# Two steps of the projections per round, in the stage that prepares the delta rule's chunks

## The chip, the cores and the metric

The kernel runs on one core of a Trainium2 chip. A core has a matrix engine (TensorE, PE in the profile), a vector engine (VectorE, DVE), a scalar engine (ScalarE, ACT), GpSimd (POOL) and a queue engine (SyncE, SP) that issues most DMAs. Each engine works through its own list of instructions in order; semaphores make an instruction wait for others. The metric is the time on the device, in microseconds (us), of one execution; a median of several is given.

## The reference

The program is one encoder layer for 1024 tokens of width 1024, with adaptive scale and shift. `hmix @ w_in` gives the inputs of three mixers: a gated short convolution (256 channels), a neighbourhood attention (4 heads of 64) and a gated delta rule in both directions (4 heads of 128). Their outputs go through `w_out`; then a router sends every token to 2 of 32 experts, and a last norm ends it. All is float32; a product that needs the precision is made of three matmuls over high and low parts.

```
proj = hmix @ w_in[l]
y_conv = cb * _dwconv(cc * cx, conv_a_w[l])
y_na = _neighbourhood_attention(...)
y_gdn = _gdn_mixer(gqkv, gz, ga, gb, ...)       # chunks, triangular solve, scan; times silu(gz)
mixed = concatenate([y_conv, y_na, y_gdn]) @ w_out[l]
x = x + gate1 * mixed
y_moe = _hier_moe(rmsnorm(x), ...)
```

The delta rule needs, per chunk, the inverse of a unit triangular matrix, and then walks over the chunks one after the other with a state, once forward and once backward.

## The kernel before

The sequence is cut into 8 chunks of 128 tokens. The stages in time: input norm and first projections; attention beside the delta rule's own projections (to about 365 us); then the stage of the change; then `w_out`, second norm and router; then, from about 860 us, the experts.

What the change touches is the list of generators at lines 806 to 815. Each generator emits some instructions and yields; one such piece is called a step here. `rounds` (line 120) goes round: one step of every generator it has, in the order given, until those named in `until` are through. What is left of the others goes on in the next call of `rounds`, at line 920.

- `prep_as` (lines 735 and 683), two generators with four chunks each, 7 steps a chunk: loads, decay matrices, norms, transposes and two products of each chunk, and stores to DRAM; the last (line 731) is the transposed triangular matrix `l_d`. So its 28 steps stand in rounds 1 to 28.
- `prj` (lines 324 and 812): the projections that are left, with weights loaded on ACT's queue and split into a high and a low part on ACT and DVE (line 62). First six conv projections (`feat`, line 334, 8 steps each with 6 matmuls of 512 columns a step, line 340), then two groups of gate inputs z, 8 steps each (`tok`, line 346), one step a chunk of 128 tokens: 24 matmuls of 256 columns (line 355) and a readout by ACT and DVE and a store (lines 505 to 507). A step of `tok` is called a token step, or token, below; there are 16. Altogether `prj` has 64 steps.
- `pcs`: two generators of `prep_c` (line 774), one over chunks 0, 1, 2, 3, the other over 7, 6, 5, 4, 11 steps a chunk. They solve the matrix from blocks of 16 up to 128 in three steps of size (line 783). Each has masks on POOL and DVE (lines 787 to 789), a product copied to `Y` by ACT (line 792), and two more products added by DVE (lines 795 and 796). Then DVE scales the result into `to` (line 801), which is stored (line 802).
- `inverses`: `prep_b` (line 745), the 16 x 16 blocks, in two halves: chunks 0, 7, 1, 6 and then 2, 5, 3, 4. On DVE (lines 759 and 761), with nine steps each. The first waits for the second chunk of `prep_as`, the second for the fourth, so that they stand in rounds 14 to 22 and 28 to 36. `prep_c` of a chunk waits for its half.

The call at line 815 ends with `inverses`, after 37 rounds. The call at line 920 goes on with the rest of `prj`, `pcs`, two `visits` (line 843, the scan, which waits for `done_c` of its chunk) and `wo_thread` (line 904). The latter scales and splits a row block of `w_out` and writes it over the tiles `hh` and `hl` that the projections read; its row k is emitted once 9 + k token steps are.

The order of the code is not yet an engine's order. A planner goes through all instructions in a simulated time of its own. Where several are ready for one engine, it takes the one that was emitted first; where none of the early ones is ready, a later one goes ahead. Tiles of a pool share a fixed number of buffers: three PSUM banks `mm` for the projections, two `t1` tiles for what is read out of them.

Of the kernel before, what the change touches and what calls it, by code (L numbers as in the profile page):

```python
# [33 lines left out]
def body(tc, I, O):  # L34
    nc = tc.nc
    with ExitStack() as ctx:
        _body(ctx, tc, nc, I, O)


def _body(ctx, tc, nc, I, O):  # L40
# [79 lines left out]
    def rounds(*threads, until=None):  # L120

        live = list(threads)
        left = list(threads if until is None else until)
        while left:
            for g in list(live):
                if next(g, live) is live:
                    live.remove(g)
                    if g in left:
                        left.remove(g)
# [7 lines left out]
    def fast(g, n):  # L137

        for i, _ in enumerate(g):
            if i % n == n - 1:  # L140
                yield
# [161 lines left out]
    def chain(*gs, every=0):  # L303

        n = 0
        for g in gs:
            for _ in g:
                n += 1
                if every and n % every == 0:
                    tick()  # L310
                yield
# [7 lines left out]
    def proj(*items, got=(), q=sp):  # L319

        todo = [spec for specs, _ in items for spec in specs]
        got = [*got] or [wload(*spec, q) for spec in todo[:2]]
        n = len(got)
        for specs, f in items:
            ws = []
            for _ in specs:
                if n < len(todo):
                    got.append(wload(*todo[n], q))
                    n += 1
                ws.append(wsplit(got.pop(0)))  # L330
            yield from f(ws)
# [403 lines left out]
    def prep_as(cs):  # L735
        d = cs[0] // 7
        nxt = prep_load(cs[0], d)
        for i, c in enumerate(cs):
            f, R = nxt
            for n in prep_a(c, f, R):  # L740
                if n and i + 1 < len(cs):
                    nxt = prep_load(cs[i + 1], d)
                yield

    def prep_b(cs):

        while not done_a.issuperset(cs):
            yield
        N = g1p.tile([P, 2, 16, 16], F32, name="N")
        for i, c in enumerate(cs):  # L750
            for a in range(2):
                sp.dma_start(N[32 * i:32 * i + 32, a], blocks(l_d[c, a]))
        W = g1p.tile([P, 2, 16, 16], F32, name="W")
        pool.memset(W, 0.0)
        Wf = W.rearrange("p a i j -> p a (i j)")
        pool.memset(Wf[:, :, 0:256:17], 1.0)
        pr = g1p.tile([P, 2, 15, 15], F32, name="prod")
        for i in range(1, 16):
            dve.tensor_tensor(pr[:, :, :i, :i], N[:, :, i, None, :i].to_broadcast([P, 2, i, i]),
                              W[:, :, :i, :i].rearrange("p a j c -> p a c j"), op=OP.mult)  # L760
            dve.tensor_reduce(W[:, :, i, :i], pr[:, :, :i, :i], axis=AX.X, op=OP.add)
            if i % 2:
                yield
        pool.memset(Wf[:, 1, 0:256:17], 0.0)
        Z = g1p.tile([P, 2, 16, 16], F32, name="Z")
        pool.tensor_add(Z[:, 0], W[:, 0], W[:, 1].rearrange("p i j -> p j i"))
        pool.tensor_add(Z[:, 1], W[:, 1], W[:, 0].rearrange("p i j -> p j i"))
        for i, c in enumerate(cs):
            for a in range(2):
                sp.dma_start(blocks(t_d[c, a]), Z[32 * i:32 * i + 32, a])  # L770
        done_b.update(cs)
        yield

    def prep_c(c):
        while c not in done_b:
            yield
        LT = gc.tile(H4, F32, name="LT")
        sp.dma_start(LT, dense(l_d[c, 1]))
        TT = gc.tile([P, 2, 4, P], F32, name="TT")
        for a in range(2):  # L780
            sp.dma_start(TT[:, a], dense(t_d[c, a]))
        yield
        for s in (16, 32, 64):
            BT = gc.tile(H4, F32, name="BT")
            D1 = gc.tile(H4, F32, name="D1")
            D2 = gc.tile(H4, F32, name="D2")
            pool.tensor_mul(BT, LT, m4(f"b{s}"))
            dve.tensor_mul(D1, TT[:, 0], m4(f"m{s}"))
            pool.tensor_mul(D2, TT[:, 1], m4(f"m{s}"))
            yield  # L790
            Y = gc.tile(H4, F32, name="Y")
            act.copy(Y, mm4(BT, D1, psc))
            yield
            if s < 64:
                dve.tensor_add(TT[:, 0], mm4(D2, Y, psc), TT[:, 0])
            dve.tensor_add(TT[:, 1], mm4(Y, D2, psc), TT[:, 1])
            yield
        for d, n in ((0, "ui"), (1, "li"))[::1 if c < 4 else -1]:
            to = gc.tile(H4, F32, name="to")
            for h in range(4):  # L800
                dve.scalar_tensor_tensor(to[:, h], TT[:, 1, h], colv[:, 2, d, h, c:c + 1], M[n], op0=OP.mult, op1=OP.mult)
            sp.dma_start(w_d[c, d], flat(to))
        done_c.add(c)
        yield
# [6 lines left out]
    inverses = chain(prep_b((0, 7, 1, 6)), prep_b((2, 5, 3, 4)))  # L811
    prj = proj(*conv, *zs, q=act)
    pcs = [chain(*(prep_c(c) for c in halves[i::2])) for i in range(2)]
    pas = [prep_as(lo), prep_as(up)]
    rounds(*pas, prj, *pcs, inverses, until=[*pas, inverses])
    qctx.close()


# [1097 lines left out]
```

## Time and profile before

| | us |
|---|---|
| median of 3 runs | 1516.59 (1515.83 to 1517.48) |
| the profiled execution | 1518.59 |
| its span | 1516.8 |
| PE, DVE, ACT, POOL busy in the span | 1355.5, 1173.4, 804.9, 424.2 |
| the stage's `prep_a`, from its first load to its last store | 367 to 530 |
| `prep_c`, from its first load of a block inverse to its last store | 505 to 673 |

The profile is of one execution. A row of the timeline has the start, the duration, engine, line, operation and tiles, and, in brackets, how long the engine had been idle and what ended that. Neighbouring rows of one kind are merged, with their count behind an x. A name with q (SPq) is an engine's queue as it issues. Matmuls overlap, so the start of the next row says more of PE than the duration does.

### The profile page before, as it was taken

What the parts mean: (1) busy time and instruction counts of PE and PEld (TensorE: products, weight loads), DVE (VectorE), ACT (ScalarE), POOL (GpSimd) and SP (SyncE); (2) the same over time, 40 slices, a digit from 0 to 9 for tenths busy, and PEclk for the clock granted to TensorE, in tenths of its full rate; (3) what the DMA queues carried; (4) which work ended last, traced back from release to release, by engine and by line L of the source; (5) the groups of instructions that cost most, each with busy time, mean ns of one, the idle gap of its engine ahead of it and who ended that gap; (6) DMA issues with size and microseconds to landing.
All of it is one profiled execution on the core that took longest, in us unless ns stands there. A gap on an engine that the chain in (4) does not pass through costs nothing. (4 is left out here: it accounts for less than half of the span.)

```text
span 1516.8 us, 21838 instructions
## 1 busy us (share of the span) xinstructions
PE 1355.5 (89%) x7239; PEld 1076.5 (71%) x7239; DVE 1173.4 (77%) x2143; ACT 804.9 (53%) x1333; POOL 424.2 (28%) x294
## 2 busy tenths in 40 slices
PE   3988999999877888869999789999999999999983
PEld 2866777777766788868877678878866776676652
DVE  6758666544547688757877789999999889978996
ACT  3633454433544222321332367778888768767873
POOL 0011311200100555633532011212236414413432
PEclk9998999999998899989999689999999999999997
DMA  9496455223788676658565779999999999989923
GB/s 340 121 198 195 149 177 166 96 74 89 204 201 210 174 195 214 192 191 273 164 246 175 305 264 372 374 352 374 359 346 391 366 393 365 377 311 320 366 82 148
DMA packets 172601, 375.75 MB, mean 248 GB/s; under 512 B 33458, under 2 KB 99634, under 8 KB 147908
## 3 DMA queue, kind: packets, MB, share of 16 engines
q1 hardware_dynamic: 162500, 351.13, 67.7%
q0 software_dynamic: 7072, 16.73, 4.7%
q10 hardware_dynamic: 2912, 6.46, 1.4%
q8 instruction: 59, 0.97, 0.3%
q14 instruction: 58, 0.48, 0.1%
HBM read 325.38 MB, written 56.80 MB: 252 GB/s over the span
## 5 line engine op out<-in xcount | busy, mean ns | idle before, releaser
L62 DVE TENSOR_TENSOR wl<-w,wh 128x1024 fp32r<-128x1024 f32 (+1 forms) x392 | 456.7, 1195 | 33.8 <-ACT wh L62 30.9
L62 ACT CAST wh<-w 128x1024 fp32r<-128x1024 f32 (+1 forms) x392 | 401.0, 1033 | 118.7 <-PE y L1357 45.6
L1445 POOL DMA_INDIRECT x_d<-yo,ixp x27 | 127.0, 4704 | 222.8 <-DVE yo L1441 214.4
L340 PE MATMUL mm<-hh,wh 128*128 128x512 f32 x352 | 148.1, 421 | 0.0
L340 PE MATMUL mm<-hh,wl 128*128 128x512 f32 x352 | 143.3, 407 | 1.4 <-DVE wl L62 1.4
L340 PE MATMUL mm<-hl,wh 128*128 128x512 f32 x352 | 143.8, 409 | 0.0
L1368 PE MATMUL h<-wl,xh 128*128 128x512 f32 x288 | 122.8, 427 | 9.0 <-DVE wl L62 7.9
L1368 PE MATMUL h<-wh,xh 128*128 128x512 f32 x288 | 113.3, 401 | 0.7 <-ACT wh L62 0.7
L1357 PE MATMUL y<-wh,uh 128*64 128x512 f32 (+1 forms) x272 | 108.2, 398 | 0.8 <-ACT uh L62 0.5
L1357 PE MATMUL y<-wh,ul 128*64 128x512 f32 (+1 forms) x272 | 107.1, 394 | 0.4 <-DVE ul L62 0.4
L1357 PE MATMUL y<-wl,uh 128*64 128x512 f32 (+1 forms) x272 | 106.3, 398 | 0.7 <-DVE wl L62 0.7
L1357 PE MATMUL h<-wh,xh 128*128 128x512 f32 x224 | 90.3, 403 | 1.0 <-ACT u L1412 0.9
L1357 PE MATMUL h<-wl,xh 128*128 128x512 f32 x224 | 89.6, 400 | 0.0
L1357 PE MATMUL h<-wh,xl 128*128 128x512 f32 x224 | 88.5, 395 | 0.8 <-DVE xl L62 0.6
L1381 POOL DMA_INDIRECT oacc<-xn_d,ixp x29 | 50.2, 1732 | 134.7 <-PE pt L1397 117.8
L1368 PEld LDWEIGHTS h<-wl,xh 128*128 128x128 f32 x288 | 54.3, 189 | 40.3 <-DVE wl L62 31.6
L340 PEld LDWEIGHTS mm<-hh,wh 128*128 128x128 f32 x352 | 68.2, 194 | 18.2 <-issue 6.9
L340 PEld LDWEIGHTS mm<-hl,wh 128*128 128x128 f32 x352 | 68.2, 194 | 15.5 <-issue 0.3
L340 PEld LDWEIGHTS mm<-hh,wl 128*128 128x128 f32 x352 | 68.2, 194 | 13.4 <-DVE wl L62 1.7
L405 POOL TENSOR_TENSOR acc<-acc,wa 128x512 f32<-128x512 f32 x28 | 40.7, 1452 | 87.2 <-ACT wa L403 48.4
L1368 PEld LDWEIGHTS h<-wh,xh 128*128 128x128 f32 x288 | 54.4, 189 | 8.8 <-ACT wh L62 1.4
L1357 PEld LDWEIGHTS y<-wl,uh 128*64 128x64 f32 (+1 forms) x272 | 42.6, 157 | 20.9 <-DVE wl L62 2.4
(440 smaller groups left out, 3138.2 us busy)
## 6 DMA issues: line engine op xcount, KB each, us to landing
w<-we SPq DMA_DIRECT2D x192, 1024.0 KB
wa<-w_ada SPq DMA_DIRECT2D x64, 256.0 KB
wa<-w_ada SPq DMA_DIRECT2D x16, 512.0 KB
wr<-w_in_f SPq DMA_DIRECT2D x16, 512.0 KB
qkv_d<-t SPq DMA_DIRECT2D x12, 512.0 KB
f<-qkv_d SPq DMA_DIRECT2D x8, 768.0 KB
t_d<-zt SPq DMA_DIRECT2D x8, 516.0 KB
xt<-x SPq DMA_DIRECT2D x8, 512.0 KB
```

The source lines that it names most:

```text
L62: return act.copy(hi, src), dve.tensor_sub(lo, src, hi.bitcast(F32))
L340: pe.matmul(ps, a[:, k], of(b, k, h * 512, 512), start=n == 0, stop=n == 3 * KT - 1)
L405: pool.tensor_add(acc, acc, w)
L1357: pe.matmul(out, a[:, k0 + k], b[:, k % 2], start=first and n == 0, stop=last and n == 11)
L1368: pe.matmul(out, xs[:, k0 + k], b[:, k % 2], start=first and n == 0, stop=last and n == 7)
L1381: return pool.indirect_dma_start(out=self.xg, out_offset=None, in_=xn_d, in_offset=bass.IndirectOffsetOnAxis(ap=self.idx()[0], axis=0), bo ...
L1445: return pool.indirect_dma_start(out=x2_d, out_offset=bass.IndirectOffsetOnAxis(ap=self.idx()[0], axis=0), in_=self.yo, in_offset=None, bo ...
```

## The change

Line 815 takes `prj` through `fast`. That generator (line 137) yields only after every second step, so that a round has two steps of `prj`:

```
def fast(g, n):

    for i, _ in enumerate(g):
        if i % n == n - 1:
            yield
```

```diff
-    rounds(*pas, prj, *pcs, inverses, until=[*pas, inverses])
+    rounds(*pas, fast(prj, 2), *pcs, inverses, until=[*pas, inverses])
```

`prj` itself is still listed in line 920. Its 64 steps take 32 rounds where line 815 has 37, so that none is left there, and `wo_thread` finds all token steps emitted from its first round on.

## Rows read from the trace of the kernel before

**Rows 1.** The page: its head.
```profile
span 1516.8 us, 21838 instructions
```

**Rows 2.** Windows: busy us of each engine, granted clock, DMA share, GB/s.
```profile
600.00:700.00 100.00, 82.28 (x613) 78.25 (x612) 70.89 (x150) 24.44 (x54) 49.27 (x46) 0.93 0.67 211
...
640.00:650.00 10.00, 7.43 (x55) 7.23 (x54) 7.36 (x10) 1.55 (x4) 4.79 (x3) 0.87 0.46 133
...
960.00:1440.00 480.00, 470.58 (x2268) 344.96 (x2266) 438.69 (x489) 370.66 (x449) 164.20 (x54) 1.00 0.99 361
```

**Rows 3.** Timeline of SP: stores of `prep_a` and `prep_c`, first expert weights.
```profile
490.44 0.36 SPq L731 DMA_DIRECT2D l_d<-R  x1
...
672.60 0.38 SPq L802 DMA_DIRECT2D w_d<-to  x1
...
761.00 1.28 SPq L1179 DMA_DIRECT2D w<-we  x3
```

**Rows 4.** Groups of instructions, PE, 483 to 505 us: the projections' matmuls.
```profile
L355 PE MATMUL mm<-wl,hh 128*128 128x256 f32 x20 | 6.7, 338 | 0.0
L355 PE MATMUL mm<-wh,hl 128*128 128x256 f32 x21 | 6.6, 321 | 0.0
L355 PE MATMUL mm<-wh,hh 128*128 128x256 f32 x20 | 6.4, 320 | 0.0
...
L340 PE MATMUL mm<-hh,wl 128*128 128x512 f32 x1 | 0.5, 480 | 0.0
```

**Rows 5.** Timeline of ACT: a readout, copies to `Y`, a cast of `w_out`.
```profile
521.46 0.67 ACT L505 ACTIVATE t<-mm 128x256 f32<-128x256 f32 x2
...
531.83 0.58 ACT L792 COPY Y<-g 128x512 f32<-128x512 f32 x1 [0.31 <-PE g L657]
...
554.34 0.59 ACT L792 COPY Y<-g 128x512 f32<-128x512 f32 x1 [0.60 <-PE g L657]
...
570.71 0.59 ACT L792 COPY Y<-g 128x512 f32<-128x512 f32 x1 [0.31 <-PE g L657]
...
592.17 0.58 ACT L792 COPY Y<-g 128x512 f32<-128x512 f32 x1 [2.22 <-PE g L657]
...
610.02 0.59 ACT L792 COPY Y<-g 128x512 f32<-128x512 f32 x1 [2.32 <-PE g L657]
...
627.61 0.59 ACT L792 COPY Y<-g 128x512 f32<-128x512 f32 x1
...
659.78 0.62 ACT L62 CAST hh<-xp 128x512 fp32r<-128x512 f32 x1 [3.59 <-POOL xp L911]
...
661.30 0.59 ACT L792 COPY Y<-g 128x512 f32<-128x512 f32 x1
```

**Rows 6.** Timeline of PE, 634 to 663 us.
```profile
642.03 1.05 PE L657 MATMUL g<-Y,D 128*128 128x128 f32 x8
642.91 1.06 PE L657 MATMUL g<-D,Y 128*128 128x128 f32 x8
...
647.55 2.08 PE L657 MATMUL g<-D,Y 128*128 128x128 f32 x8 [2.57 <-DVE TT L795]
...
652.05 0.29 PE L355 MATMUL mm<-wh,hl 128*128 128x256 f32 x1
652.17 0.28 PE L355 MATMUL mm<-wl,hh 128*128 128x256 f32 x1
...
655.60 1.95 PE L657 MATMUL g<-D,BT 128*128 128x128 f32 x16
```

**Rows 7.** Timeline of DVE: last sum of a pair, scaling, splits of `w_out`.
```profile
532.90 0.69 DVE L796 TENSOR_TENSOR TT<-g,TT 128x512 f32<-128x512 f32 x1 [2.13 <-PE g L657]
...
545.39 0.34 DVE L801 SCALAR_TENSOR_TENSOR to<-TT,cols,masks 128x128 f32<-128x128 f32 x1
...
586.55 2.57 DVE L62 TENSOR_TENSOR hl<-xp,hh 128x512 fp32r<-128x512 f32 x2
...
650.35 3.31 DVE L62 TENSOR_TENSOR hl<-xp,hh 128x512 fp32r<-128x512 f32 x2
```

## The prediction

> **What bounds the kernel now.** The first view to read is the page's head: one execution spans 1516.8 us [rows 1]. The stretches come next: from 960 us on the DMA engines are 0.99 busy, and that part begins when the expert weights start to load. Those loads are issued first at 761.00 [rows 3], right behind the delta rule's last visit, so whatever ends earlier or later before 761 moves the whole rest with it. Between 600 and 700 no engine is full: PE 82 us of 100, DVE 71, ACT 24, POOL 49 [rows 2]. So that stretch is a chain of waits, not a full engine, and the chain is found by following tiles in order of time. The last chunk pair's solved matrix is stored at 672.60 [rows 3], and only then can the fourth of the eight visits in each direction start. Hence the end of `prep_c` (lines 774 to 804) sets the end of the kernel.
>
> `prep_c` solves four chunk pairs one after the other (0/7, 1/6, 2/5, 3/4), each in three steps. Every step has one ACT copy into `Y` (line 792), so these copies are the chain's clock. For the later of the two chains [rows 5]: pair 0/7 makes its third copy at 531.83; pair 1/6 its first at 554.34 and third at 570.71; pair 2/5 at 592.17 and 610.02; pair 3/4 at 627.61 and 661.30. From a pair's first to its third copy that is 16.4, 17.9 and 33.7 us; from third copy to the next pair's first 22.5, 21.5 and 17.6 us. The last pair is slow, and PE's order there says why.
>
> **What decides the order.** An instruction emitted earlier goes first where the planner finds two ready on one engine. I count emission in rounds of line 815 (line 920 carries the count on). `prep_a` takes rounds 1 to 28, pair 0/7 23 to 33, 1/6 34 to 44, 2/5 45 to 55, 3/4 56 to 66. In the kernel before, step p of `prj` stands in round p: the 48 steps of the six conv projections, then the 16 z tokens (line 355) in rounds 49 to 64, with the eight `w_out` rows (`wo_thread`) in 57 to 64. PE's timeline agrees: token matmuls run in one block (two of them at 652.05 and 652.17), and pair 3/4's third product (round 64) starts right behind its last, at 655.60 [rows 6]. A token that stands earlier in the order makes a chain wait.
>
> **The change part by part.** Nothing is added or removed; 64 steps and eight rows move. With two steps a round `prj` is through in round 32: tokens 1 and 2 stand in round 25, tokens 15 and 16 in round 32, and the `w_out` rows in rounds 38 to 45.
>
> *Up to about 505 us: nothing.* `prep_a` passes round 21 at 490.44, with the store of its third chunk [rows 3], while the last matmuls of the conv projections (step 48, round 24 at two a round) run just behind 483 [rows 4]: PE had already filled its gaps with them far ahead of their rounds. Even at two a round `prep_a` stands earlier in the order there, so I take 0. The bounds are -5 and +5, one matrix split or conv group on DVE either way.
>
> *From 505 to 563: the tokens come before pair 0/7 (a loss).* At 505, 61 token matmuls are done (20, 21 and 20 of the three kinds) [rows 4]; 384 - 61 = 323 are left. Two that follow each other start 0.12 us apart (652.05, 652.17 [rows 6]), so they are 38 us of PE at full clock. In the trace they fill waits until 655. Now tokens up to 8 come before pair 0/7's second product (round 28), up to 14 before its third (31), and all 16 before its last (32). PE must also run what still precedes that: a group of 8 starts 0.9 us before the next one (642.03, 642.91 [rows 6]). For each of two threads that is two groups of 8 and two of 4 of `prep_a` (2.7 us) and 7 groups of `prep_c` (6.3 us), together 18 us. 505 + 38 + 18 = 561, and pair 0/7's last sum, made at 532.90 [rows 7], comes at about 562. Cost +29. The bounds are 0 (tokens only fill waits, as now) and +35 (the splits of the two late z weights, some 5 us, keep PE idle as well). I take 29, because the block before 655.60 shows the order being kept.
>
> *From pair 0/7 to 1/6 and 2/5 (a gain).* Behind pair 0/7 the scaling on DVE lasts from 533 to 545.39, since the second inverse runs among it [rows 7]; after the change that inverse is over by then. Behind pair 1/6 two splits of `w_out` (2.57 us at 586.55 [rows 7]) stand before the next pair's first mask. Both transitions can come down to the third one's 17.6: -4.9 and -3.9.
>
> *Pair 3/4 (a gain).* No token and no `w_out` row is left. Its 33.7 us can come down to 17.1, the mean of the two pairs before: -16.6. The rows say what goes: the token block before 655.60, a 3.31 us split at 650.35 [rows 7], and ACT's 3.59 us wait for `w_out` at 659.78, behind which two `Y` copies were queued, the later at 661.30 [rows 5]. What is late next is the chain's own latency.
>
> *The `w_out` rows (a loss).* They write over tiles that the tokens read, so they follow tokens 9 to 16 and end near 580, in pair 1/6's transition. Four rows are eight splits, some 10 us of DVE; most lies beside DMA waits. I charge +3, one split before a mask as at 650.35; bounds 0 and +10.
>
> *DMA queues.* The z stores and the w_in_z loads move with the tokens, past the second inverse's loads on SP's queue. SP only issues here, 0.3 to 0.6 us each; 0, bounds -3 and +3.
>
> Sum: 29 - 4.9 - 3.9 - 16.6 + 3 = +6.6 us. The profiled execution took 1518.59, so it would take 1525.2; the median of the runs shown is 1516.59, 2.0 lower, which gives 1523.
>
> **A rule weighed against the rows.** After 2.57 us without work PE's group of 8 at 647.55 took 2.08 us, where the one at 642.91 took 1.06 [rows 6]; the mean granted clock of 640 to 650 is 0.87 [rows 2]. That is 1.2 in place of 2.4 GHz. The Trainium skill (TensorE: Matmul & The Clock Gate, section "HAM oscillation — how this bites in real kernels") says that bursts between waits each start throttled again; the trace agrees at this place. It speaks against the change, which takes out of the three later transitions the tokens that keep PE busy there. It is rival three.
>
> **The rivals.**
> *One, faster (0.30): the tokens pace themselves.* A token needs one of three PSUM banks and one of two `t1` tiles, which come free only after a store on SP's queue. For: the 61 matmuls done at 505 are two tokens and a half [rows 4], yet ACT read two tokens out at 521.46 only [rows 5]. If that lasts, PE stalls on the tokens and runs pair 0/7 in between. It decides at a loss of 22 us in pair 0/7 (25.4 - 3): below that the change wins. With a third of the 29 lost, 10 us, the sum is 10 - 25.4 + 3 = -12: 1504. Against: in the new order the stores move forward too.
> *Two, no difference (0.20).* Loss and gain cancel to 3 us, since both are the same 38 us of tokens on another pair; 1517.
> *Three, the clock (0.10).* With three transitions empty, some four groups of 8 in each run at half speed: 3 x 4 x 1.0 = 12 us on top of the sum; 1535.
> The forecast itself: 0.40.
>
> **How the numbers follow.** Slower is the forecast and rival three, 0.50; same 0.20; faster 0.30. About 0.2% (3 us) is what a measurement of this kernel can tell from no change. The likeliest case's own range is 1520 to 1536 (its unknown terms, +35 for +29 and +10 for +3, against a lighter lock). The full range reaches to rival one until some 1 in 10 is left out at each end: 1504 to 1536.
>
> **What would show it.** Right: token matmuls in near unbroken runs from about 505 to 560, the last of them near 560, not 655; pair 0/7's third `Y` copy near 555; pair 3/4's first-to-third copy 17 us; the last store of `to` 5 to 10 us later than 672.6, and the first expert weight later than 761 by as much. Wrong: pair 0/7's third copy before 550 (rival one); chain groups in the transitions at twice 0.9 us (rival three); a `prep_a` that passes round 21 more than 5 us away from 490; or a first expert weight that doesn't follow the last store of `to`.

## The result, and the profile after

The changed kernel is slower. Its median is 1536.43 us (1534.99 to 1537.66, four runs), that of the kernel before, run beside it, 1516.21 (1514.83 to 1517.48): +20.2 us, a ratio of 1.0135 [1.0115, 1.0154]. The forecast was 1523 us (+6.6) with a range of 1504 to 1536. The profiled execution took 1535.57 us, with a span of 1533.8; that of the kernel before took 1518.59, 17.0 less.

The page's head and its busy times after the change: no engine's busy time has moved by more than 8 us (DVE's, by 7.5), so most of the 20 us are waits.

```profile
span 1533.8 us, 21843 instructions
PE 1356.6 (88%) x7239; PEld 1075.6 (70%) x7239; DVE 1180.9 (77%) x2143; ACT 805.6 (53%) x1333; POOL 424.5 (28%) x294
```

ACT's timeline after, the rows of the later chain's copies into `Y` that answer to [rows 5] (where a row has x2, it is the second of the two, so the third copy of pair 0/7 comes at 565.3):

```profile
533.83 1.21 ACT L792 COPY Y<-g 128x512 f32<-128x512 f32 x2
...
564.84 1.06 ACT L792 COPY Y<-g 128x512 f32<-128x512 f32 x2
...
580.86 1.14 ACT L62 CAST hh<-xp 128x512 fp32r<-128x512 f32 x2 [10.48 <-POOL xp L911]
...
594.49 0.59 ACT L792 COPY Y<-g 128x512 f32<-128x512 f32 x1 [1.92 <-PE g L657]
...
609.71 0.59 ACT L792 COPY Y<-g 128x512 f32<-128x512 f32 x1 [0.31 <-PE g L657]
...
627.72 0.59 ACT L792 COPY Y<-g 128x512 f32<-128x512 f32 x1
...
644.68 0.59 ACT L792 COPY Y<-g 128x512 f32<-128x512 f32 x1 [1.73 <-PE g L657]
...
660.25 0.59 ACT L792 COPY Y<-g 128x512 f32<-128x512 f32 x1 [0.54 <-PE g L657]
...
679.13 0.59 ACT L792 COPY Y<-g 128x512 f32<-128x512 f32 x1 [1.73 <-PE g L657]
```

Read against [rows 5] the copies give the whole stage:

| us | before | after | change | forecast |
|---|---|---|---|---|
| third copy of pair 0/7 | 531.8 | 565.3 | +33.5 | +29 |
| to the first of pair 1/6 | 22.5 | 29.2 | +6.7 | -4.9 |
| pair 1/6, first to third | 16.4 | 15.2 | -1.1 | 0 |
| to the first of pair 2/5 | 21.5 | 18.0 | -3.5 | -3.9 |
| pair 2/5 | 17.9 | 17.0 | -0.9 | 0 |
| to the first of pair 3/4 | 17.6 | 15.6 | -2.0 | 0 |
| pair 3/4 | 33.7 | 18.9 | -14.8 | -16.6 |
| `w_out` rows, as a term of their own | | | | +3 |
| sum: third copy of pair 3/4 | 661.3 | 679.1 | +17.8 | +6.6 |

SP's queue after, the rows that answer to [rows 3] (the store of round 21, the last stores of `to`, the first expert weights), and between them two of the `w_out` rows' loads:

```profile
488.36 0.38 SPq L731 DMA_DIRECT2D l_d<-R  x1
...
573.85 0.43 SPq L910 DMA_DIRECT2D xp<-w_out  x1
574.85 0.38 SPq L910 DMA_DIRECT2D xp<-w_out  x1
576.47 1.64 SPq L781 DMA_DIRECT2D TT<-t_d  x2
...
688.20 1.40 SPq L802 DMA_DIRECT2D w_d<-to  x2
...
776.95 1.28 SPq L1179 DMA_DIRECT2D w<-we  x3
```

Round 21 is passed 2.1 us earlier than before, the last `to` store is issued 16.7 us later (689.3 against 672.60), the first expert weight 15.9 us later.

Two windows after (columns as in [rows 2]). In the first PE is near full, with 293 of the 384 token matmuls (130 in the same stretch before). In the second, behind them, it works 18 us of 40, at a granted clock of 0.70:

```profile
505.00:565.00 60.00, 54.72 (x447) 53.56 (x446) 49.69 (x89) 16.28 (x33) 24.69 (x16) 0.97 0.62 187
560.00:600.00 40.00, 17.87 (x129) 17.25 (x129) 29.56 (x50) 8.82 (x18) 21.36 (x14) 0.70 0.49 138
```

The second window in the kernel before:

```profile
560.00:600.00 40.00, 35.52 (x289) 34.39 (x288) 32.41 (x67) 12.55 (x26) 22.64 (x17) 0.96 0.70 202
```

What PE does there, after: the last token matmul at 564.18 (the block of [rows 6] stood before 655.60), pair 0/7's last products behind it, and then nothing for 20.61 us:

```profile
564.18 0.28 PE L355 MATMUL mm<-wh,hh 128*128 128x256 f32 x1
565.56 2.02 PE L657 MATMUL g<-D,Y 128*128 128x128 f32 x16 [1.11 <-ACT Y L792]
588.20 2.04 PE L657 MATMUL g<-D,BT 128*128 128x128 f32 x8 [20.61 <-DVE D L788]
590.03 1.91 PE L657 MATMUL g<-wv,wt 128*128 128x128 f32 x8
592.35 2.05 PE L657 MATMUL g<-D,BT 128*128 128x128 f32 x8 [0.41 <-DVE D L788]
594.19 1.13 PE L657 MATMUL g<-Y,D 128*128 128x128 f32 x8
```

DVE in that gap, after, and POOL's row that DVE's wait leads to:

```profile
566.77 1.87 DVE L911 TENSOR_TENSOR xp<-xp,g1row 128x1024 f32<-128x1024 f32 x1
569.33 2.66 DVE L62 TENSOR_TENSOR hl<-xp,hh 128x512 fp32r<-128x512 f32 x2 [0.68 <-ACT hh L62]
...
572.57 0.68 DVE L796 TENSOR_TENSOR TT<-g,TT 128x512 f32<-128x512 f32 x1
...
581.51 3.84 DVE L62 TENSOR_TENSOR hl<-xp,hh 128x512 fp32r<-128x512 f32 x2 [5.27 <-ACT hh L62]
585.27 2.18 DVE L801 SCALAR_TENSOR_TENSOR to<-TT,cols,masks 128x128 f32<-128x128 f32 x8
587.37 0.68 DVE L788 TENSOR_TENSOR D<-TT,emasks 128x512 f32<-128x512 f32 x1
```

```profile
578.49 4.64 POOL L911 TENSOR_TENSOR xp<-xp,g1row 128x1024 f32<-128x1024 f32 x2 [7.05 <-DMA xp<-w_out]
```

From 565 on this is a queue, not a full engine. Pair 0/7's sum (572.57) stands behind the product of one `w_out` row with `g1row` (566.77) and behind a split (569.33). The second chain's scaling into `to` (585.27) and the next pair's first mask (587.37) stand behind the split at 581.51, which waits for ACT's cast (580.86), that for POOL's product (578.49), and that for a `w_out` load which SP issued only at 573.85. Nothing of this is needed by pair 1/6; it is only ahead of it on DVE.

### The profile page after: what moved, and what is told of

Its sections match the earlier page's. It is cut to its first block, busy times and chain, and to the rows that moved or that the text cites. A ratio compares the mean times of both kernels' runs of the same rounds, so it can differ in the third digit from the quotient of the medians.

```text
span 1533.8 us, 21843 instructions
## 1 busy us (share of the span) xinstructions
PE 1356.6 (88%) x7239; PEld 1075.6 (70%) x7239; DVE 1180.9 (77%) x2143; ACT 805.6 (53%) x1333; POOL 424.5 (28%) x294
## 5 line engine op out<-in xcount | busy, mean ns | idle before, releaser
L340 PEld LDWEIGHTS mm<-hl,wh 128*128 128x128 f32 x352 | 68.3, 194 | 15.7 <-issue 0.3
```

The costliest lines, as they stand in the source:

```text
L340: pe.matmul(ps, a[:, k], of(b, k, h * 512, 512), start=n == 0, stop=n == 3 * KT - 1)
```

## The experiments

Three theories were to be told apart. *Lock*: the tokens' PE time stands before pair 0/7. *Rows*: the `w_out` rows, now at the seam of pairs 0/7 and 1/6, cost there what the forecast had counted as gained at pair 3/4. *Clock*: PE's gaps cost through the granted clock. In all diffs `rnd[0]` counts rounds, and `paced(g, when)` emits step p of a generator no sooner than round `when(p)`. On the chips of these runs the early part ended later than in the first profiles (the store of round 21 by 2 to 8 us), so times in the stage are told from the store of `prep_a`'s last `l_d` (530.5 before, 527.0 after). By that measure the last store of `to` comes 142.1 us behind it before and 162.3 after, +20.2; that this is the change of the median too is chance. Every such figure is from one profiled execution, and the first run below, whose order hardly differs from the changed kernel's, gives 165.7 for 162.3: a single figure holds to some 3 us.

**The rows held back by emission.** On the changed kernel:

```
-            while len(z_done) < NT + k + 1:
+            while len(z_done) < NT + k + 1 or rnd[0] < 57 + k:
```

> The changed kernel, with w_out row k held back to round 57 + k, where it stood before the change; the tokens stay early. Theory (the w_out rows lengthened the step from pair 0/7 to pair 1/6): the distance from pair 0/7's third Y copy to pair 1/6's first falls from 28.6 us to 18 to 22; pair 3/4's first to third copy grows again from 18.9 to 23 to 28, since the rows now lie there; time 1525 to 1533. Rival (the tokens alone made that step long, by what they leave undone on DVE): the distance stays at 26 us or more, and the time is 1536 or above.

Measured: 1541.63 against 1518.81, ratio 1.0153 [1.0114, 1.0192]. Pair 0/7 to 1/6 took 27.7 us (after 29.2). But the rows had not moved: their loads went out from 406.6 to 581.3, after the change from 402.0 to 574.8. The planner lets a later instruction go first where no early one is ready, so rank alone did not hold them. The rival's numbers came, but as the rows stayed in their place, this run decides nothing between rows and tokens.

**Only the conv projections at two a round**, tokens in their old rounds, on the kernel before:

```
+    prj = ...; rnd[0] = 0; prj = paced(prj, lambda p: (p + 1) // 2 if p <= 48 else p)
```

> Half of the change: the six conv projections at two steps a round (through in round 24), the 16 tokens in rounds 49 to 64 as before the change, and so the w_out rows too. Theory (only the tokens' place matters, the conv projections ran ahead of their rounds anyway): 1511 to 1521, pair 0/7's third copy within 5 us of 531.8. Rival (the doubled conv steps take DVE and ACT from prep_a): prep_a's last store later than 530 by 5 us or more and 1522 to 1530.

Measured: 1521.57, ratio 1.0012 [0.9986, 1.0038]; pair 0/7's third copy 2.8 us behind `prep_a`, before 1.3, and the last `to` store 140.2, before 142.1. The absolute times lie between theory and rival (third copy at 540.8, `prep_a`'s last store at 538.0), but 4.8 us of that were there at round 21 already; the ratio and the distances show no effect of this half of the change. The loss is with the other half, the tokens and what follows them.

**Short tokens**, on the changed kernel:

```
-            for k in range(KT):
+            for k in (0, KT - 1):
...
-                    pe.matmul(ps[:, :n_], ..., start=n == 0, stop=n == 3 * KT - 1)
+                    pe.matmul(ps[:, :n_], ..., start=n == 0, stop=n == 5)
```

> The changed kernel with 6 of the 24 matmuls in each token step; it leaves 3/4 of the z projection's sums out, readouts, stores and splits stay. Theory (the lock on pair 0/7 is PE time of tokens): 14 tokens x 18 matmuls x 0.118 us = 30 us less PE work ahead of pair 0/7's last product, its third copy comes at 535 to 545 in place of 565.9, time 1500 to 1515. Rival (the lock is the tokens' readouts, stores and splits, or the planner's order as such): third copy after 555, time above 1525.

Its total, 1596.0 us, can't be compared: with other data the router sends tokens elsewhere, and the experts load 196 weights, not 192. So the times of theory and rival stay unanswered. The stage can be compared. Pair 0/7's third copy comes 12.7 us behind `prep_a` (545.69 - 533.0) where it was 38.3 with whole tokens: 25.6 us of the lock went with three quarters of the token matmuls. Behind the first profile's `prep_a` that would be 539.7, within the 535 to 545 of the theory. So the lock is for the most part the tokens' own time. Yet the stage's end comes 150.4 us behind `prep_a`, 8.3 more than before with a quarter of the token matmuls: pair 1/6 took 23.4 us, with the rows beside it.

**The chains at two a round from line 920 on**, tokens as before:

```
-    wot = wo_thread()
+    wot, pcs = wo_thread(), [fast(g, 2) for g in pcs]
```

> The kernel before, with two steps a round for the two chains of prep_c in the second call of rounds, so that pairs 2/5 and 3/4 come before the tokens and the w_out rows. Theory (in the kernel before, tokens 13 to 16 and w_out rows cost pair 3/4 some 15 us): pair 3/4's first to third copy falls from 33.7 to 16 to 20 us and the time to 1500 to 1511. Rival (the late tokens and w_out rows then end the stage themselves): the copy distance falls, but the time is 1514 or more.

Measured: pair 3/4 takes 15.6 us, and the last `to` store comes 113.4 us behind `prep_a`, 28.7 sooner than before. The time stays, as the rival had it: 1521.61, ratio 1.0016 [0.9996, 1.0036]. The rows of the experts' loads and of the product with `w_out` (by source line; the times are those of the first and the last) say why:

```profile
L1179 SPq DMA_DIRECT2D w<-we x192: 328/333/733, 737.1 to 1438.3; - x192
...
L964 PE MATMUL po<-hh,fh x64: 392/396/796, 691.1 to 828.3; 128*128 128x512 f32 x64
L964 PE MATMUL po<-hl,yh x64: 388/394/628, 739.3 to 849.7; 128*128 128x512 f32 x64
```

and in the kernel before, with the last product of the visits (`vn`, `wm`) and the registers that line 1179 sets for expert loads:

```profile
L964 PE MATMUL po<-hl,yh x64: 389/395/482, 717.7 to 844.1; 128*128 128x512 f32 x64
L657 PE MATMUL g<-vn,wm x128: 271/275/348, 566.9 to 760.6; 128*128 128x128 f32 x128
L1179 SPq FUSED_REGOPS  x174: 46/46/56, 880.5 to 1430.5; - x174
```

The first expert weight is 24 us earlier than before, but the first `w_out` product is 10 us later (before 681.4) and the last one 6 us later: the tokens, pushed back, run until 684.4 (before 655.5), the rows' loads until 682.1. The visits end at 736.7, 24 us sooner, and the last product stands 113 us behind them, where it is 83 before the change and after it. What the end goes with is the last `w_out` product: the cast of the experts' order (line 1326) follows it by 33.8 us here, by 35.2 before (879.3) and by 35.0 after the change, and the end of the span follows that cast by 637 to 639 us in all three. 174 of the 192 expert loads wait for that order, and their registers are set only behind the cast; the other 18 came sooner here, and the time stayed. In the other runs the cast follows the last product by 33.6 to 37.6 us, with one exception of 41.7 (both at two a round), but the first product by 195 to 214. The last product needs the last visit, and it needs the rows, which follow the tokens.

**Rows behind pair 1/6's loads**, on the changed kernel:

```
+            tt_of[c] = sp.dma_start(TT[:, a], dense(t_d[c, a]))
...
+            with tc.issue_after(tt_of[6 if k > 1 else 0].ins): sp.dma_start(w, ...)
```

> The changed kernel, with the loads of w_out rows 2 to 7 put behind pair 1/6's last load of a block inverse on SP's queue, so that their splits can't stand before pair 0/7's end. PE's order stays. Theory (w_out rows made pair 0/7's end and the transition late): pair 0/7's third copy unchanged against prep_a, the distance from it to pair 1/6's first falls from 28.6 to 17 to 21 us; the rows then cost pair 1/6 up to 6; the ratio to the kernel before falls from 1.0135 to 1.004 to 1.010. Rival (the transition is long for the tokens' sake): it stays at 26 or more and the ratio at 1.012 or more.

Rows 0 and 1 moved as well, behind pair 0/7's loads. Measured: the transition went from 29.2 to 23.6 us and the third copy of pair 0/7 from 38.3 to 31.1 behind `prep_a`, 12.8 us together. Pair 1/6 then took 22.5 (after 15.2), and the next transition 27.0 (after 18.0). Ratio 1.0159 [1.012, 1.0198], no gain: the theory's transition (17 to 21) and ratio were both missed. The rows' cost went along with the rows.

**Tokens one a round, from round 25**:

```
+    prj = ...; rnd[0] = 0; prj = paced(prj, lambda p: (p + 1) // 2 if p <= 48 else p - 24)
```

> The conv projections at two steps a round as in the changed kernel, the 16 tokens at one a round from round 25 on, so that pair 0/7's last product has 8 tokens before it, not 16. Theory (the loss is the PE time of the tokens ahead of it): its third copy comes 20 to 28 us earlier, measured from prep_a's last store (38.9 us in the changed kernel, 1.3 in the kernel before: 11 to 19 here); pair 1/6 loses up to 10 to tokens 9 to 16; ratio 1.000 to 1.009. Rival (any token ahead of the chains costs the same): third copy 33 or more behind that store, ratio 1.012 or more.

Measured: the third copy comes 8.9 us behind `prep_a` (11 to 19 expected), but pair 1/6 takes 37.0 us. Ratio 1.0134 [1.0107, 1.016], as slow as the change, where the theory had 1.000 to 1.009. In time the tokens' price stays the same and is paid at another pair. By the stage's measure it is smaller: the last `to` store comes 154.6 us behind `prep_a`, between 142.1 and 162.3.

**Both at two a round**, chains too, in both calls, on the changed kernel:

```
-    rounds(*pas, fast(prj, 2), *pcs, inverses, until=[*pas, inverses])
+    rounds(*pas, fast(prj, 2), *fpcs, inverses, until=[*pas, inverses])
```

> The changed kernel with the two chains of prep_c at two steps a round as well, in both calls. Theory (what counts is the chains' place against the tokens): pair 0/7 stands in rounds 23 to 28, its third copy has 6 tokens before it and comes within 12 us of prep_a's last store; tokens 7 to 16 and the w_out rows fall to pairs 1/6 and 2/5; ratio 0.992 to 1.005. Rival (two steps a round of the projections cost by themselves): 1.010 or more.

Measured: ratio 1.0122 [1.0094, 1.015], the rival's side. Pair 0/7's third copy is 2.5 us ahead of `prep_a`'s end, but that end itself comes 51.5 us behind the store of round 21 (before 40.0). Pair 1/6 takes 43.8 us, and the second inverse works on DVE until 584.7 (after 565.0). **The same with tokens from round 33**:

```
+    prj = ...; rnd[0] = 0; prj = paced(prj, lambda p: (p + 1) // 2 if p <= 48 else p - 16)
```

> A version meant to be better than both: conv projections at two steps a round, tokens at one a round in rounds 33 to 48, the chains of prep_c at two. Theory (the end is the later of the chains' and the w_out rows' end, plus a fixed rest): both end 5 to 15 us before the kernel before, ratio 0.990 to 0.998. Rival (the stage's sum of work, not its order, is what is left): 0.998 to 1.004.

Measured: ratio 1.0098 [1.0072, 1.0125], slower than theory and rival. Pair 2/5 makes its first copy only at 609.5, behind an inverse stored at 600.0 (after 573.2). In the first of the two the tokens' time moved to what stood next, pair 1/6 (token matmuls run until 600.5); in the second, what of the wait for the inverse is theirs isn't told apart.

The second run also refutes its theory of the end. Its last `to` store comes at 672.4 and its first `w_out` product at 680.2, both no later than before (672.6 and 681.4), and its last row is loaded at 627.4. Yet it is 15.9 us slower. Its visits end 19 us later than before, and with them the last product comes 13 us later:

```profile
L657 PE MATMUL g<-vn,wm x128: 271/275/422, 576.1 to 780.0; 128*128 128x128 f32 x128
L964 PE MATMUL po<-hl,yh x64: 388/394/484, 727.3 to 856.8; 128*128 128x512 f32 x64
```

**The rows out of the stage, in either order.** The same hold on both kernels: rows emitted when all chunks are solved, their loads behind the last `to` store.

```
-            while len(z_done) < NT + k + 1:
+            while len(z_done) < NT + k + 1 or len(done_c) < NT:
...
+            with tc.issue_after(to_of[4].ins): sp.dma_start(w, ...)
```

> The changed kernel with all w_out rows behind the chains: emitted after the last prep_c, and their loads behind chunk 4's last store on SP's queue. Read in the stage, from prep_a's last store to the last store of prep_c: 162.3 us in the changed kernel, 142.1 in the kernel before. Theory (the rows cost the chains some 15 us wherever they lie among them, which the forecast left out): 144 to 150, with pair 0/7's third copy 30 to 33 behind prep_a and pair 1/6's first 18 to 23 behind that. Rival (the tokens alone lengthen the stage): 156 or more. The time as a whole gets worse in both, to 1545 to 1570, since the w_out product waits for the rows.

> The same hold of the w_out rows in the kernel before. Theory (there too the rows, not the tokens, are most of what pair 3/4 loses): the stage from prep_a's last store to the last store of prep_c falls from 142.1 to 124 to 132 us and pair 3/4's first to third copy from 33.7 to 17 to 23. Rival (the tokens are what pair 3/4 loses): 136 or more, and 27 or more. Time 1530 to 1550.

SP's timeline of the changed kernel with the rows last (the last store of `l_d` is the second of the pair, at 529.3; the last of `to` at 680.1):

```profile
528.78 0.99 SPq L731 DMA_DIRECT2D l_d<-R  x2
...
677.37 3.01 SPq L802 DMA_DIRECT2D w_d<-to  x2
```

and of the kernel before with the rows last (the last of `to` at 668.6):

```profile
537.75 0.49 SPq L731 DMA_DIRECT2D l_d<-R  x1
...
666.17 2.71 SPq L802 DMA_DIRECT2D w_d<-to  x2
```

| from `prep_a`'s end to the last `to`, us | rows in the stage | rows last | rows cost |
|---|---|---|---|
| order before | 142.1 | 130.8 | 11.3 |
| order after | 162.3 | 150.8 | 11.5 |
| the tokens' order costs | 20.2 | 20.0 | |

150.8 is just past the 144 to 150 that was expected of it, 130.8 within its 124 to 132. Within the 3 us or so that one execution allows, the rows cost the chains the same in both orders, and what the tokens' order costs without them is the whole difference. Told from the store of round 21 instead, the rows cost 11.6 and 13.6 us and the order 18.8 and 16.7. The runs' times agree: 1551.97 with the tokens forward and 1535.74 with them as before, 16.2 us apart, beside one kernel before of 1519.63 (ratios 1.0213 [1.0189, 1.0237] and 1.0098 [1.0073, 1.0123]). Both are slower than with the rows inside, since the product now waits for the rows.

ACT's timeline of the two shows where those 20 us sit. Changed kernel, rows last, pair 0/7's third copy and pair 1/6's first:

```profile
562.37 0.59 ACT L792 COPY Y<-g 128x512 f32<-128x512 f32 x1 [0.30 <-PE g L657]
...
582.74 0.59 ACT L792 COPY Y<-g 128x512 f32<-128x512 f32 x1 [1.51 <-PE g L657]
```

Kernel before, rows last, the same two and pair 3/4's first and third:

```profile
539.52 0.59 ACT L792 COPY Y<-g 128x512 f32<-128x512 f32 x1 [0.31 <-PE g L657]
...
562.20 0.59 ACT L792 COPY Y<-g 128x512 f32<-128x512 f32 x1 [0.96 <-PE g L657]
...
634.72 0.58 ACT L792 COPY Y<-g 128x512 f32<-128x512 f32 x1
...
658.59 0.59 ACT L792 COPY Y<-g 128x512 f32<-128x512 f32 x1 [0.31 <-PE g L657]
```

From `prep_a`'s end to the third copy: 33.1 and 1.8 us, a lock of 31.3. The transition: 20.4 and 22.7. Pair 3/4: 19.0 (650.8 to 669.7) and 23.9 (just past its 17 to 23), a gain of 4.9.

**Chains three steps in two rounds**, on the kernel before:

```
-    wot = wo_thread()
+    wot, pcs = wo_thread(), [(0 for i, _ in enumerate(g) if i % 3 != 1) for g in pcs]
```

> The kernel before with three steps in two rounds for the chains of prep_c in the second call. Theory (the end is the later of two: the first w_out product plus 195 us, and the last visit plus 118; with chains at two a round the visits ended 29 us earlier and the w_out rows too late): both come 5 to 10 us earlier, ratio 0.993 to 0.998. Rival (the w_out product can't start earlier, whatever the chains do): 0.999 to 1.004.

Measured: 1527.85, ratio 1.0055 [1.0037, 1.0072]; the last `to` store at 664.0, the last token at 673.5, the last row's load at 672.2, the first product at 685.7. Slower; both expectations were missed.

**Chains at two a round from line 920, tokens from round 41**, on the kernel before:

```
+    prj = ...; rnd[0] = 0; prj = paced(prj, lambda p: (p + 1) // 2 if p <= 48 else p - 8)
...
+    wot, pcs = wo_thread(), [fast(g, 2) for g in pcs]
```

> Chains of prep_c at two steps a round in the second call, conv projections at two a round, tokens at one a round in rounds 41 to 56 and the w_out rows behind them in 49 to 56. Theory as for the last run: the first w_out product comes 8 to 20 us earlier than with the chains alone made fast, ratio 0.988 to 0.997. Rival: the tokens take from the chains what they gain, 0.999 to 1.006.

Measured: 1511.62 (1509.6 to 1516.71) against 1519.63, ratio 0.994 [0.992, 0.9959]: faster than both kernels, by the theory's numbers. `prep_c` and the rows now end together: the last `to` store at 656.5, the last `w_out` load at 661.4, and the first product at 681.3, as before, though `prep_a` had ended 5.0 us later (535.5 against 530.5):

```profile
L964 PE MATMUL po<-hh,fh x64: 391/397/774, 681.3 to 822.0; 128*128 128x512 f32 x64
L964 PE MATMUL po<-hl,yh x64: 388/394/628, 715.6 to 841.9; 128*128 128x512 f32 x64
```

Its visits end at 744.6 and its first expert weight comes at 745.0, both 16 us sooner than before; its last product is 2 us sooner (841.9 against 844.1).

## Why the prediction was right or wrong

*The direction and the mechanism were right.* "A token that stands earlier in the order makes a chain wait": between 505 and 565 PE was busy for 54.7 of 60 us, with 293 token matmuls where it had run 130, the last token matmul came at 564.18, pair 0/7's third copy at 565.3, and the loss was +33.5 against +29, inside the bound of +35. With the rows away the same lock measures 31.3, and with short tokens most of it goes. Rival one, tokens that pace themselves, needed a third copy before 550. The sign "third `Y` copy near 555" doesn't follow from the prediction's own +29, which puts it at 561.

*"Up to about 505 us: nothing" was right.* Round 21 moved by 2.1 us, within the bounds, and the conv half alone gives 1.0012 [0.9986, 1.0038].

*"Pair 3/4 (a gain)" had nearly its size, -14.8 against -16.6, and named both causes, but didn't tell them apart.* Without the rows the tokens' leaving is worth 4.9 us. The `w_out` rows made up 9.8 (33.7 to 23.9 in the order before, when they go last), which [rows 5] and [rows 7] show at ACT's wait and the split. That part did not go, it moved.

*The step that failed is "The `w_out` rows (a loss)", the term +3.* In their new place they cost 11.5 us: 5.2 at the end of pair 0/7 (38.3 against 33.1 with the rows last; by which path is not shown), 8.8 in the transition to 1/6 (29.2 against 20.4), less 2.6 in the next (18.0 against 20.6). The prediction put them in pair 1/6's transition, took most of their DVE work to lie beside DMA waits, and charged one split. In fact the sixth row's product and split stood ahead of pair 0/7's sum, and the seventh's split, with DVE's wait for its load, ahead of the next pair's first mask. With this fell "Both transitions can come down to the third one's 17.6": the first was forecast at -4.9 and came to +6.7. The 8.5 us by which the term was too small (11.5 for 3) make up most of the 11.2 by which +17.8 stands over +6.6. The other 2.7 is what is left of smaller errors: without the rows' share both transitions gave less than forecast (-2.1 and -0.9 for -4.9 and -3.9) and pair 3/4 gave 1.8 less, while the three rows of the table taken as 0 gave 4.0. Put rightly, the rows are zero in the sum, 11.3 us before and 11.5 after, and the tokens alone make +20: lock 31.3, transition -2.3, pair 3/4 -4.9, the rest -4.1.

*Rival three, the clock, came in part, and that its 1535 is near the result is luck.* Its sign was seen: groups of 8 at half speed in all three later transitions. Three stand in the first, behind 20.61 us without work (2.04, 1.91 and 2.05 us, that is 1.2 GHz; the next, at 594.19, took 1.13, 2.4 GHz), three in the second and some two in the third:

```profile
619.07 2.07 PE L657 MATMUL g<-S,q 128*128 128x128 f32 x8 [1.23 <-ACT oacc L871]
620.95 2.04 PE L657 MATMUL g<-wv,wt 128*128 128x128 f32 x8
622.79 1.91 PE L657 MATMUL g<-D,BT 128*128 128x128 f32 x8
...
655.71 2.04 PE L657 MATMUL g<-wv,wt 128*128 128x128 f32 x8
```

That is some eight groups where rival three counted twelve, and the kernel before had some three in the same transitions:

```profile
546.70 2.04 PE L657 MATMUL g<-D,BT 128*128 128x128 f32 x8 [1.70 <-DVE D L788]
...
578.95 1.95 PE L657 MATMUL g<-S,q 128*128 128x128 f32 x8 [2.09 <-DVE wv L863]
```

At 1.0 us each (2.04 against 1.06) the change added some 5 us of PE time, not 12, and the second and third transition still came out shorter (-3.5 and -2.0). No run holds the clock apart from the order, so what part of the 5 us the chain paid is not shown. The Trainium skill (TensorE: Matmul & The Clock Gate, section "HAM oscillation — how this bites in real kernels") says that work after a long enough gap starts throttled; the rows agree, and in the first transition the gap itself, 20.61 us, cost seven times as much as the 3 us of its slow groups.

*"Whatever ends earlier or later before 761 moves the whole rest" held for this change and not in general.* Last `to` store +16.7, last visit +15.9 (760.6 to 776.6), first expert weight +15.9, last `w_out` product +16.0 (844.1 to 860.0), the cast of the experts' order +15.7 (879.3 to 895.0). But `prep_c` done 28.7 us sooner left the time where it was, and `prep_c` done at the same time, with visits that end 19 us later, made it 15.9 us longer. What sets the end is the last `w_out` product, which waits for the visits as well as for the rows behind the tokens. In the kernel before and in the changed one it comes 83 us behind the last visit in both, so there `prep_c` counts, through the visits.

Open: why the visits fall behind when the chains run at two a round in both calls (they end at 777.3 and 780.0). In the second of the two DVE works between 736.9 and 747.0 on the norm behind the `w_out` product, with waits for POOL, before the visits' next row; whether their place in the order does that was not tested. And the rows' cost was measured for all eight together, not row by row.

## What to carry to other kernels

Work that is pulled forward in the order of emission can cost most of its engine time at the chain it now precedes (here 31 us of some 38 for the 16 tokens, 20 net), and work that drags behind it has to be charged at its new place before its old place is booked as a gain. Find the instruction where several threads meet, and ask which is late there: of the versions tried, only the one that brought the solved chunks and the `w_out` rows to the `w_out` product together was faster. A cheap instruction that waits for a DMA can cost the chain behind it the wait too, not only its own duration: here DVE's wait of 5.27 us and the split of 3.84 behind it are about the 8.8 us that the rows cost the transition.

## What the runs showed of the hardware

DVE, ACT and POOL each stood still in turn for one DMA: from 573.85, when the load was issued, to 581.51, when DVE's split began, with an idle DVE of 5.27 us, an idle ACT of 10.48 and an idle POOL of 7.05 before their rows, and a pair's scaling queued behind it.
